# RMS normalization on one core: squares four rows at a time, half of the rows scaled on ScalarE and multiplied on GpSimd, and the code of two engines placed at slot 60

## Chip, cores and metric

One core of a Trainium2 chip; the program is started on that core alone. The metric is device microseconds of one execution. Kernels that are compared ran on the same chip in alternating rounds.

## The reference

```python
batch, seq, dim = 16, 1024, 512            # x: float32; gamma: ones(512)
rms = np.sqrt(np.mean(x ** 2, axis=-1, keepdims=True) + 1e-5)
return (x / rms * gamma).astype(np.float32)
```

That is 16384 rows of 512 numbers: 33.55 MB to read and 33.55 MB to write. Every row is touched once, and the arithmetic is small.

## The kernel before

The rows are cut into 4 tiles of 128 partitions x 32 rows (8.39 MB each), which live in three buffers ("slots" in the kernel's names, not to be confused with the code slots of the change). Eight rows (a group) are worked on at a time. All loads and stores of x are issued from SyncE, in this order; each covers all 128 partitions:

```python
    load(0, 0, 0, 8); load(0, 0, 8, 16); load(0, 0, 16, 32); load(1, 1, 0, 32)
    ...
    def transfers(t, g):                    # called after a group is done
        if (t, g) == (0, 0):
            store(0, 0, 0, 1)               # one-row stores between the loads of tile 2
            load(2, 2, 0, 16)
            store(0, 0, 1, 2)
            load(2, 2, 16, 24)
            store(0, 0, 2, 3)
            load(2, 2, 24, 32)
        elif (t, g) == (0, 24):  store(0, 0, 3, 32)
        elif (t, g) == (1, 8):   store(1, 1, 0, 16); load(3, 0, 0, 16); load(3, 0, 16, 32)
        elif (t, g) == (1, 24):  store(1, 1, 16, 32)
        elif (t, g) == (2, 24):  store(2, 2, 0, 32)
        elif (t, g) == (3, 8):   store(3, 0, 0, 16)
        elif (t, g) == (3, 24):  store(3, 0, 16, 32)
```

So there are 18 transfers of x. The arithmetic of a group:

```python
    # row_stats: sums of squares; two kinds of group alternate
    #   odd groups:  ScalarE squares 4 rows into PSUM, VectorE reduces them    (x2)
    #   even groups: ScalarE squares one row and accumulates its sum           (x8)
    nc.scalar.activation(out=rms, in_=ss, func=AF.Sqrt, bias=eps_t, scale=1.0 / D)
    nc.vector.reciprocal(out=rstd, in_=rms)
    # apply: for each of the 8 rows, on VectorE: row = row * rstd * gamma
    nc.vector.scalar_tensor_tensor(out=..., in0=..., scalar=rstd[:, r : r + 1],
                                   in1=gamma_b, op0=OP.mult, op1=OP.mult)
```

Of the kernel before, what the change touches and what calls it, by code (L numbers as in the profile page):

```python
# [1 line left out]

# [4 lines left out]


@with_exitstack
def kernel(  # L10
    ctx: ExitStack,
    tc: tile.TileContext,
    x: bass.AP,
    gamma: bass.AP,
    out: bass.AP,
):
    nc = tc.nc
    P = nc.NUM_PARTITIONS
    eps = 1e-5
    fp32 = mybir.dt.float32  # L20
    AF = mybir.ActivationFunctionType
    OP = mybir.AluOpType

    xf = x.flatten_outer_dims()
    of = out.flatten_outer_dims()
    N, D = xf.shape
    R = 32
    G = 8
    H = 4
    assert N == 4 * P * R  # L30

    xv = xf.rearrange("(t p r) d -> t p r d", p=P, r=R)
    ov = of.rearrange("(t p r) d -> t p r d", p=P, r=R)

    const = ctx.enter_context(tc.tile_pool(name="const", bufs=1))
    stats = ctx.enter_context(tc.tile_pool(name="stats", bufs=4))
    psum = ctx.enter_context(tc.tile_pool(name="psum", bufs=2, space=bass.MemoryType.PSUM))

    slots = [const.tile([P, R, D], fp32, name=f"slot{i}") for i in range(3)]

    def load(t, slot, r0, r1):
        nc.sync.dma_start(out=slots[slot][:, r0:r1], in_=xv[t][:, r0:r1])

    def store(t, slot, r0, r1):
        nc.sync.dma_start(out=ov[t][:, r0:r1], in_=slots[slot][:, r0:r1])

    load(0, 0, 0, 8)
    load(0, 0, 8, 16)
    load(0, 0, 16, 32)
    load(1, 1, 0, 32)  # L50

    gamma_row = const.tile([1, D], fp32)
    nc.scalar.dma_start(out=gamma_row, in_=gamma.unsqueeze(0))
    ones_col = const.tile([1, P], fp32)
    nc.vector.memset(ones_col, 1.0)  # L55
    gamma_psum = psum.tile([P, H, D], fp32, name="sq")
    nc.tensor.matmul(gamma_psum[:, 0], ones_col, gamma_row, start=True, stop=True)  # L57
    gamma_b = const.tile([P, D], fp32)
    nc.vector.tensor_copy(out=gamma_b, in_=gamma_psum[:, 0])  # L59

    eps_t = const.tile([P, 1], fp32)
    nc.vector.memset(eps_t, eps)  # L62
    sq_scratch = const.tile([P, D], fp32)

    def row_stats(slot, g):
        ss = stats.tile([P, G], fp32, name="ss")
        rms = stats.tile([P, G], fp32, name="rms")
        rstd = stats.tile([P, G], fp32, name="rstd")
        if (g // G) % 2:
            for h in range(0, G, H):  # L70
                sq = psum.tile([P, H, D], fp32, name="sq")
                nc.scalar.activation(out=sq, in_=slots[slot][:, g + h : g + h + H, :], func=AF.Square)  # L72
                nc.vector.tensor_reduce(  # L73
                    out=ss[:, h : h + H], in_=sq, axis=mybir.AxisListType.X, op=OP.add
                )
        else:
            for r in range(G):
                nc.scalar.activation(  # L78
                    out=sq_scratch,
                    in_=slots[slot][:, g + r, :],  # L80
                    func=AF.Square,
                    accum_out=ss[:, r : r + 1],
                )
        nc.scalar.activation(out=rms, in_=ss, func=AF.Sqrt, bias=eps_t, scale=1.0 / D)  # L84
        nc.vector.reciprocal(out=rstd, in_=rms)  # L85
        return rstd

    def apply(slot, g, rstd):
        for r in range(G):
            nc.vector.scalar_tensor_tensor(  # L90
                out=slots[slot][:, g + r, :],
                in0=slots[slot][:, g + r, :],
                scalar=rstd[:, r : r + 1],
                in1=gamma_b,
                op0=OP.mult,
                op1=OP.mult,
            )

    groups = [(t, g) for t in range(4) for g in range(0, R, G)]
    slot_of = [0, 1, 2, 0]  # L100

    def transfers(t, g):
        if (t, g) == (0, 0):
            store(0, 0, 0, 1)
# [5 lines that stand above are left out]
        elif (t, g) == (0, 24):  # L110
            store(0, 0, 3, 32)
        elif (t, g) == (1, 8):
            store(1, 1, 0, 16)
            load(3, 0, 0, 16)
            load(3, 0, 16, 32)
        elif (t, g) == (1, 24):
            store(1, 1, 16, 32)
        elif (t, g) == (2, 24):
            store(2, 2, 0, 32)
        elif (t, g) == (3, 8):  # L120
            store(3, 0, 0, 16)
        elif (t, g) == (3, 24):
            store(3, 0, 16, 32)

    ahead = row_stats(0, 0)
    for k, (t, g) in enumerate(groups):
        rstd = ahead
        if k + 1 < len(groups):
            tn, gn = groups[k + 1]
            ahead = row_stats(slot_of[tn], gn)  # L130
        apply(slot_of[t], g, rstd)
        transfers(t, g)


# [1 line left out]
_INS = ['x', 'gamma']  # L136
_OUTS = [((16, 1024, 512), 'float32')]


# [23 lines left out]
```

## Time and profile before

| | before |
|---|---|
| time, median of 3 runs | 162.62 us (162.05 to 162.84) |
| span of the profiled run | 160.3 us |
| VectorE / ScalarE busy | 122.6 us (76%) / 80.1 us (50%) |
| data moved | 67.11 MB, 97.8% of the 16 DMA engines' time |

97.8% of 160.3 us is 156.8 us for each DMA engine on average. The kernel moves data nearly all the time, and no arithmetic can help unless a transfer waits for it.

The costliest groups of instructions (line, engine, operation, shapes, count; then busy us and mean ns of one; then idle time just before):

```profile
L90 DVE SCALAR_TENSOR_TENSOR slot<-slot,rstd,gamma_b 128x512 f32<-128x512 f32 x128 | 85.7, 738 | 0.1
L78 ACT ACTIVATE sq_scratch<-slot 128x512 f32<-128x512 f32 x64 | 40.0, 625 | 16.0 <-DMA slot<-in_x_dram 14.7
L73 DVE TENSOR_REDUCE ss<-sq 128x4 f32<-128x2048 f32 x16 | 36.0, 2274 | 10.1 <-ACT sq L72 10.0
L72 ACT ACTIVATE sq<-slot 128x2048 f32<-128x2048 f32 x16 | 29.8, 1862 | 8.1 <-DVE ss L73 8.1
```

What SyncE waited for when it issued transfers (total us, times, longest):

```profile
SPq L45 <- DVE slot L90: 102.3, 5, 27.5
SPq L158 <- DMA out_dram<-slot: 16.4, 1, 16.4
...
```

The second of these lines is the wait from the last store's issue to its landing. It is much longer than the store itself needs (4.19 MB are 9.8 us at 428 GB/s, which is 67.11 MB in the 156.8 us), so an earlier store was still under way: the arithmetic is several us ahead of the DMA even at the end.

The last stretches of the span, with the busy time of each engine (all zero by then), and in the last two columns the DMA share and GB/s. A packet is counted here in the stretch in which it starts.

```profile
core 0: us, PE busy (x) PEld busy (x) DVE busy (x) ACT busy (x) POOL busy (x), PEclk, DMA share, GB/s
157.50:158.00 0.50, 0.00 (x0) 0.00 (x0) 0.00 (x0) 0.00 (x0) 0.00 (x0) 1.00 0.16 66
158.00:158.50 0.50, 0.00 (x0) 0.00 (x0) 0.00 (x0) 0.00 (x0) 0.00 (x0) 1.00 0.01 0
158.50:159.00 0.50, 0.00 (x0) 0.00 (x0) 0.00 (x0) 0.00 (x0) 0.00 (x0) 1.00 0.00 0
159.00:160.00 1.00, 0.00 (x0) 0.00 (x0) 0.00 (x0) 0.00 (x0) 0.00 (x0) 1.00 0.00 0
```

After 158.0 us no data packet starts any more.

### The profile page before, as it was taken

How to read it: one execution, taken by the hardware profiler on the slowest of the kernel's cores; microseconds unless marked ns; L12 is line 12 of the kernel's file. 1: busy time of each engine (PE TensorE's matmuls, PEld its weight loads, DVE VectorE, ACT ScalarE, POOL GpSimd, SP SyncE). 2: the span in 40 equal slices, each digit the busy share in tenths (PEclk: the TensorE clock that was granted, in tenths of full speed). 3: DMA queues.
4: the chain of work that ended last, by engine and by line, in shares of the span. 5: the costliest groups of instructions: out<-in, count | busy, mean ns of one | idle time of the engine just before them, and what ended most of it. 6: DMA issues, size and time to landing. Idle time of an engine off the chain costs nothing.

```text
span 160.3 us, 415 instructions
## 1 busy us (share of the span) xinstructions
PE 2.0 (1%) x2; PEld 0.5 (0%) x2; DVE 122.6 (76%) x163; ACT 80.1 (50%) x162; POOL 0.2 (0%) x4
## 2 busy tenths in 40 slices
PE   4000000000000000000000000000000000000000
PEld 1000000000000000000000000000000000000000
DVE  0102999999995199999999999999999999950000
ACT  3099739900499999969009600796099400000000
POOL 0000000000000000000000000000000000000000
DMA  6999999969799999998899999999999799799993
GB/s 197 437 413 523 392 392 523 523 262 523 327 403 407 456 435 503 474 444 356 385 441 466 401 409 490 401 401 499 409 515 474 327 507 458 335 392 450 458 401 139
DMA packets 2597, 67.13 MB, mean 419 GB/s; under 512 B 290, under 2 KB 290, under 8 KB 675
## 3 DMA queue, kind: packets, MB, share of 16 engines
q1 hardware_dynamic: 2592, 67.11, 97.8%
q14 instruction: 3, 0.02, 0.0%
q10 hardware_dynamic: 2, 0.00, 0.0%
HBM read 33.56 MB, written 33.55 MB: 419 GB/s over the span
## 4 chain that ended last, share of the span: by engine, by line
DVE 69%; ACT 12%; DMA 4%; issue 2%; DVEq 0%
DVE slot L90 51%; DVE ss L73 17%; ACT sq_scratch L78 7%; ACT sq L72 4%; DMA slot<-in_x_dram 4%; DVE rstd L85 1%; ACT rms L84 1%; DVEq L158 0%
## 5 line engine op out<-in xcount | busy, mean ns | idle before, releaser
L90 DVE SCALAR_TENSOR_TENSOR slot<-slot,rstd,gamma_b 128x512 f32<-128x512 f32 x128 | 85.7, 738 | 0.1
L78 ACT ACTIVATE sq_scratch<-slot 128x512 f32<-128x512 f32 x64 | 40.0, 625 | 16.0 <-DMA slot<-in_x_dram 14.7
L73 DVE TENSOR_REDUCE ss<-sq 128x4 f32<-128x2048 f32 x16 | 36.0, 2274 | 10.1 <-ACT sq L72 10.0
L72 ACT ACTIVATE sq<-slot 128x2048 f32<-128x2048 f32 x16 | 29.8, 1862 | 8.1 <-DVE ss L73 8.1
L84 ACT ACTIVATE rms<-ss,eps_t 128x8 f32<-128x8 f32 x16 | 4.6, 298 | 26.6 <-DVE ss L73 26.4
L78 ACT ACTIVATION_READ_ACCUMULATOR sq_scratch<-slot 128x1 f32 x64 | 11.9, 187 | 0.0
L85 DVE RECIPROCAL rstd<-rms 128x8 f32<-128x8 f32 x16 | 3.1, 192 | 5.7 <-ACT rms L84 5.7
L59 DVE COPY gamma_b<-sq 128x512 f32<-128x512 f32 x1 | 0.7, 692 | 3.2 <-PE sq L57 3.2
L57 PE MATMUL sq<-gamma_row,ones_col 1*128 1x512 f32 x2 | 2.0, 1122 | 2.1 <-DMA gamma_row<-in_gamma_dram 2.1
L78 ACT ACT_TABLE_LOAD x1 | 1.3, 1283 | 1.3 <-PEq L147 1.3
L84 ACT ACT_TABLE_LOAD x1 | 1.3, 1283 | 0.0
L55 DVE MEMSET ones_col<- 1x128 f32 x1 | 0.2, 165 | 0.8 <-PEq L147 0.8
L57 PEld LDWEIGHTS sq<-gamma_row,ones_col 1*128 1x128 f32 x2 | 0.5, 306 | 2.1 <-issue 2.1
L147 POOL MEMSET const-bfloat16-1.0<- 128x1 bf16 x1 | 0.1, 101 | 0.0
L147 POOL MEMSET const-uint8-127<- 128x1 uint8 x1 | 0.1, 101 | 0.0
L147 POOL MEMSET const-float32-0.0<- 128x1 f32 x1 | 0.1, 98 | 0.2 <-issue 0.2
L147 POOL MEMSET const-float32-1.0<- 128x1 f32 x1 | 0.1, 98 | 0.0
L62 DVE MEMSET eps_t<- 128x1 f32 x1 | 0.1, 59 | 0.0
## 6 DMA issues: line engine op xcount, KB each, us to landing
slot<-in_x_dram SPq DMA_DIRECT2D x4, 4096.0 KB, 24.7
out_dram<-slot SPq DMA_DIRECT2D x4, 4096.0 KB, 22.5
slot<-in_x_dram SPq DMA_DIRECT2D x4, 2048.0 KB, 11.5
out_dram<-slot SPq DMA_DIRECT2D x1, 7424.0 KB, 35.8
out_dram<-slot SPq DMA_DIRECT2D x3, 256.0 KB, 32.1
gamma_row<-in_gamma_dram ACTq DMA_DIRECT2D x1, 2.0 KB
slot<-in_x_dram SPq DMA_DIRECT2D x1, 40.0
out_dram<-slot SPq DMA_DIRECT2D x1
```

Of the source, the lines that this page charges most:

```text
L55: nc.vector.memset(ones_col, 1.0)
L57: nc.tensor.matmul(gamma_psum[:, 0], ones_col, gamma_row, start=True, stop=True)
L59: nc.vector.tensor_copy(out=gamma_b, in_=gamma_psum[:, 0])
L62: nc.vector.memset(eps_t, eps)
L72: nc.scalar.activation(out=sq, in_=slots[slot][:, g + h : g + h + H, :], func=AF.Square)
L73: nc.vector.tensor_reduce(out=ss[:, h : h + H], in_=sq, axis=mybir.AxisListType.X, op=OP.add)
L78: nc.scalar.activation(out=sq_scratch, in_=slots[slot][:, g + r, :], func=AF.Square, accum_out=ss[:, r : r + 1],)
L84: nc.scalar.activation(out=rms, in_=ss, func=AF.Sqrt, bias=eps_t, scale=1.0 / D)
L85: nc.vector.reciprocal(out=rstd, in_=rms)
L90: nc.vector.scalar_tensor_tensor(out=slots[slot][:, g + r, :], in0=slots[slot][:, g + r, :], scalar=rstd[:, r : r + 1], in1=gamma_b, op0=O ...
L147: nc = _bacc.Bacc("TRN2", target_bir_lowering=False, num_devices=1)
```

## The change

Its intent was to relieve VectorE, the busiest compute engine: ScalarE scales half of the rows and GpSimd multiplies those by gamma; in exchange all sums of squares come from four-row squares on ScalarE and reductions on VectorE. VectorE reads gamma from PSUM, so that it has one SBUF input only. Two lines also ask for a place for the code of ScalarE and VectorE; "slot 60" below is only a name for their argument `offset=60`, and so for other numbers.

```diff
+    nc.scalar.addr_align(128, offset=60, max_nops=0)
+    nc.vector.addr_align(128, offset=60, max_nops=0)
 ... (PSUM buffers, gamma kept in PSUM and in SBUF)
-        if (g // G) % 2: ... else: ...          # two kinds of group
+        for h, home in ((0, psum), (H, const)):
+            sq = home.tile([P, H, D], fp32, name=f"sq{h}")
+            nc.scalar.activation(out=sq, in_=slots[slot][:, g + h : g + h + H, :], func=AF.Square)
+            nc.vector.tensor_reduce(out=ss[:, h : h + H], in_=sq, axis=mybir.AxisListType.X, op=OP.add)
 ...
-        for r in range(G):
+        for r in range(H):
+            nc.scalar.activation(
+                out=x[:, g + r, :], in_=x[:, g + r, :], func=AF.Copy, scale=rstd[:, r : r + 1]
+            )
+        nc.gpsimd.tensor_tensor(
+            out=x[:, g : g + H, :], in0=x[:, g : g + H, :],
+            in1=gamma_b.to_broadcast([P, H, D]), op=OP.mult,
+        )
+        for r in range(H, G):
             nc.vector.scalar_tensor_tensor(
 ...
-                in1=gamma_b,
+                in1=gamma_psum,
```

The 18 transfers of x stay as they were, in the same order.

## The prediction

> **What bounds the kernel now.** The DMA engines. The page's DMA queue part gives queue 1 67.11 MB and 97.8% of 16 engines' span: 0.978 x 160.3 = 156.8 us. The packets in the trace run from about 2.5 us after the span's start to its end, so inside that stretch under 1 us is empty. 67.11 MB in 156.8 us is 428 GB/s[...]. VectorE is 122.6 us busy (76%) and ScalarE 80.1 (50%). The chain of waits is 69% VectorE, but it ends at the last store's issue: in the timeline VectorE ends at 142.5 us, and the waits of the DMA queue show 16.4 us from there to landing. The last store, 4.19 MB, needs only 9.8 us at 428 GB/s, so its data began to move near 150: about 7 us of slack, even at the end.

> **What the change does, costed from the trace.**
> - All squares become 128x2048: 32 x 1.86 us, minus about 0.06 overlap, = 58 us. The 64 ACTIVATEs with accumulator read (64 x 0.75 pitch = 48 us) go. Added: 64 scaled copies of 128x512, estimated 0.65 us each = 41 us. ScalarE: 80 -> about 103 us.
> - VectorE: 16 more reduces of 2.24 us (+36), 64 fewer scalar_tensor_tensor of 0.66 us pitch (-43). 122.6 -> about 116 us. Hardly relieved.
> - GpSimd: 16 multiplies of 128x2048. No duration in the trace; [...]
> - Code placement: off the limit, worth about nothing.
> - DMA: the same 18 transfers in the same order, same sizes.

> **On the critical path: nearly nothing.** Per group (4.19 MB in and out, 9.8 us of DMA) VectorE needs 2 x 2.24 + 0.19 + 4 x 0.66 = 7.3 us, ScalarE about 6.5[...]; all below 9.8. [...] My hand schedule: first rows stored at about 25 us (20.5 before; the loads alone keep the queue full to about 40), tile 0's rest at 47 (45.8), first half of tile 1 at 65 (69), last store issued at about 140 (136 to 146), before the queue empties near 150. So the end does not move.

> **Prediction: 162.4 us, range 161.8 to 163.0.** Faster by over 2%: 0.01. Within 2%: 0.95. Slower by over 2%: 0.04.

> **What would show each step.** Queue 1 again near 156.8 us (97 to 98%) and no empty slice in the DMA row; span 160 to 160.7; VectorE busy 113 to 119, ScalarE 98 to 108[...] us; scalar_tensor_tensor and reduce means unchanged within 5% [...]; the last store issued before 149 us, with the wait from it to landing longer than 9.8 us.

> **What would make it wrong.** GpSimd at 9 us or more per multiply, or GpSimd and VectorE blocking each other so that a group takes over about 8.2 us: then stores come late, the queue runs dry and time grows by several us. In-order waits on ScalarE (scaled copies standing ahead of the next squares) could do the same. [...]

The sum came to nothing added: the terms for a group, 7.3 us for VectorE and about 6.5 us for ScalarE, were all put below the 9.8 us of DMA, so the prediction is the time of before, 162.4 us against 162.62. The 0.65 us of a scaled copy is the author's estimate; the trace of before has 625 ns for an ACTIVATE of the same 128x512 shape. The waits on ScalarE that it feared were small in after: its scaled copies waited 12.2 us in all for rstd, 2.4 us at most.

## More of the kernel before

All runs told of here are at a granted clock of 1.00.

From the page of the profile. The first line is the span. The row DMA has one digit for each fortieth of the span: the mean busy share of the 16 DMA engines in tenths. The queue lines give packets, MB, and the time of the packets as a share of 16 engines' span; queue 1 carries x, and queue 14 is of the kind that the page calls "instruction": its packets are taken here for fetches of the engines' own code.

```profile
span 160.3 us, 415 instructions
...
DMA  6999999969799999998899999999999799799993
...
q1 hardware_dynamic: 2592, 67.11, 97.8%
q14 instruction: 3, 0.02, 0.0%
...
```

At the start, from the timeline (start us, duration us): ScalarE issues the small load of gamma and loads its function table.

```profile
0.72 0.51 ACTq L53 DMA_DIRECT2D gamma_row<-in_gamma_dram  x1
...
1.27 1.28 ACT L78 ACT_TABLE_LOAD   x1 [1.27 <-PEq L147]
...
```

## The result

| | before | after |
|---|---|---|
| time, median of 4 runs | 162.34 us (161.92 to 162.84) | 164.29 us (163.91 to 164.58) |
| span of the profiled run | 160.3 us | 162.5 us |
| VectorE busy | 122.6 us | 115.5 us |
| ScalarE busy | 80.1 us | 105.2 us |
| GpSimd busy | 0.2 us | 72.5 us |

The ratio of after to before is 1.0118, with a 95% interval of 1.0078 to 1.0157: slower by about 1.2%, clear of noise, and outside the range of the prediction. A ratio is always the mean time of one kernel's fast runs over that of the other's of the same rounds, so it is not quite the ratio of the medians quoted beside it.

The page of after:

```profile
span 162.5 us, 360 instructions
...
DMA  6999999999798999999899999999999998899980
...
q1 hardware_dynamic: 2592, 67.11, 96.7%
q14 instruction: 4, 0.03, 0.1%
...
```

Queue 1 moved the same bytes in the same number of packets. Its share of the span fell from 97.8% to 96.7%, because the span grew: 96.7% of 162.5 us is 157.1 us, against 156.8. The DMA row ends in a 0 where it ended in a 3: the last fortieth of the span is nearly empty. Queue 14 has 4 packets where it had 3; one of the 3 is a packet of 32 bytes at the very start, so the 8192-byte packets, of which more below, went from 2 to 4.

The groups of after:

```profile
L88 POOL TENSOR_TENSOR slot<-slot,gamma_b 128x2048 f32<-128x2048 f32 x16 | 72.3, 4525 | 65.9 <-ACT slot L85 64.2
L72 DVE TENSOR_REDUCE ss<-sq 128x4 f32<-128x2048 f32 x32 | 71.3, 2266 | 8.6 <-ACT sq L71 8.6
L71 ACT ACTIVATE sq<-slot 128x2048 f32<-128x2048 f32 x32 | 59.9, 1883 | 8.5 <-DMA slot<-in_x_dram 6.7
L85 ACT ACTIVATE slot<-slot,rstd 128x512 f32<-128x512 f32 x64 | 40.8, 709 | 12.2 <-DVE rstd L79 12.2
L95 DVE SCALAR_TENSOR_TENSOR slot<-slot,rstd,gamma_psum 128x512 f32<-128x512 f32 x64 | 43.5, 740 | 0.2
```

VectorE's arithmetic went as costed: the reduce takes 2266 ns (2274 before) and the scalar_tensor_tensor 740 ns (738 before). GpSimd's multiply takes 4525 ns, and ScalarE's scaled copies took more than costed, 709 ns against an estimate of 650. GpSimd did not slow VectorE's scalar_tensor_tensor: 57 of the 64 instructions of after ran beside a GpSimd multiply and took 740 ns, as did the other 7. Whether gamma's place in PSUM has a part in that was not shown: no run has it elsewhere beside GpSimd's work.

SyncE's waits of after:

```profile
SPq L48 <- DVE slot L95: 72.3, 5, 16.8
SPq L48 <- POOL slot L88: 34.1, 7, 17.3
SPq L165 <- DMA out_dram<-slot: 22.4, 1, 22.4
...
```

The wait from the last store's issue to its landing is now 22.4 us (16.4 before): the arithmetic finished even further ahead of the DMA, and the kernel still ended later. So the last store did not come late. The end of the DMA work is what changed. The last stretches of after, same columns:

```profile
157.50:158.00 0.50, 0.00 (x0) 0.00 (x0) 0.00 (x0) 0.00 (x0) 0.00 (x0) 1.00 0.30 131
158.00:158.50 0.50, 0.00 (x0) 0.00 (x0) 0.00 (x0) 0.00 (x0) 0.00 (x0) 1.00 0.01 0
158.50:159.00 0.50, 0.00 (x0) 0.00 (x0) 0.00 (x0) 0.00 (x0) 0.00 (x0) 1.00 0.15 66
159.00:160.00 1.00, 0.00 (x0) 0.00 (x0) 0.00 (x0) 0.00 (x0) 0.00 (x0) 1.00 0.08 33
```

Here is the loss. After 158.0 us nearly everything is over, as before, but two more packets start. Such a packet is 32768 bytes and takes 1.21 us; one packet in a stretch of 1 us makes 1.21 / 16 = 0.08 of 16 engines, as the last line shows. So one DMA engine of the 16 still starts packets when the other fifteen have none left to start.

The packets in the trace say it exactly. Each transfer ends with a 4-byte packet on each of the 16 engines, and the last 16 of these are the moments at which the 16 engines finished (us, from the first instruction):

```
          first   median   third-last   second-last   last     last - median
before   157.82   158.05      158.34        158.43   158.96       0.92
after    158.06   158.23      158.79        159.18   161.06       2.83
```

The median engine moved by 0.18 us, the last one by 2.10 us. The spans of these two runs differ by 2.15 us.

Packets do not carry the number of their engine, but the recorded start of most packets lies 3 to 4 ns before the recorded end of another. I read the two as neighbours on one engine, and so most of them can be strung together: 2592 / 16 = 162 packets of x for each engine. The string that ends last in after, compared with the median engine after the same transfer:

```
us       what happens on this engine                                behind the median by
 3.82    8192-byte packet of queue 14, 0.31 us;
         the data packet after it takes 0.53 us longer                 0.91 us
39.9     64 KB packet at the turn from loads to stores takes
         1.20 us longer (0.31 to 0.66 on the other engines)            1.69 us
51.4     32 KB packet takes 0.59 us longer                             2.18 us
67.64    8192-byte packet of queue 14, 0.31 us;
         the data packet after it takes 0.37 us longer                 2.85 us
end                                                                   2.83 us
```

Two fetches of instructions fell on one DMA engine. In before there are also two such packets, at 45.8 and 59.8 us, but on two different engines. In after there are four: 1.8, 3.8, 67.6 and 70.3 us. The other two, at 1.8 and 70.3 us, also fell on one engine, and it ended only 0.94 us behind: it was 0.34 us behind after the first load, where the engine above was 0.91.

At the start of after, the timeline shows that ScalarE takes 2.83 us to issue the gamma load and gets to its function table at 4.02 us instead of 1.27:

```profile
1.17 2.83 ACTq L56 DMA_DIRECT2D gamma_row<-in_gamma_dram  x1
...
4.02 1.28 ACT L71 ACT_TABLE_LOAD   x1 [4.02 <-issue]
...
```

### The profile page after: what moved, and what is told of

Its sections match the earlier page's. It is cut to its first block, busy times and chain, and to the rows that moved or that the text cites. A ratio compares the mean times of both kernels' runs of the same rounds, so it can differ in the third digit from the quotient of the medians.

```text
span 162.5 us, 360 instructions
## 1 busy us (share of the span) xinstructions
PE 2.0 (1%) x2; PEld 0.5 (0%) x2; DVE 115.5 (71%) x115; ACT 105.2 (65%) x114; POOL 72.5 (45%) x20
## 3 DMA queue, kind: packets, MB, share of 16 engines
q1 hardware_dynamic: 2592, 67.11, 96.7%
## 4 chain that ended last, share of the span: by engine, by line
DMA 42%; DVE 24%; ACT 10%; issue 3%; POOLq 3%; POOL 3%; ACTq 0%; SPq 0%
DMA out_dram<-slot 23%; DMA slot<-in_x_dram 20%; DVE ss L72 15%; DVE slot L95 8%; ACT sq L71 5%; ACT slot L85 4%; POOLq L165 3%; POOL slot L88 3%; ACT L78 1%; DVE rstd L79 0%; ACTq L165 0%; SPq L45 0%; ACT rms L78 0%; ACTq L71 0%; POOLq L88 0%
## 5 line engine op out<-in xcount | busy, mean ns | idle before, releaser
L88 POOL TENSOR_TENSOR slot<-slot,gamma_b 128x2048 f32<-128x2048 f32 x16 | 72.3, 4525 | 65.9 <-ACT slot L85 64.2
L72 DVE TENSOR_REDUCE ss<-sq 128x4 f32<-128x2048 f32 x32 | 71.3, 2266 | 8.6 <-ACT sq L71 8.6
L71 ACT ACTIVATE sq<-slot 128x2048 f32<-128x2048 f32 x32 | 59.9, 1883 | 8.5 <-DMA slot<-in_x_dram 6.7
L85 ACT ACTIVATE slot<-slot,rstd 128x512 f32<-128x512 f32 x64 | 40.8, 709 | 12.2 <-DVE rstd L79 12.2
L95 DVE SCALAR_TENSOR_TENSOR slot<-slot,rstd,gamma_psum 128x512 f32<-128x512 f32 x64 | 43.5, 740 | 0.2
L62 DVE COPY gamma_b<-gamma_psum 128x512 f32<-128x512 f32 x1 | 0.7, 692 | 8.6 <-PE gamma_psum L60 8.6
L60 PE MATMUL gamma_psum<-gamma_row,ones_col 1*128 1x512 f32 x2 | 2.0, 1122 | 8.1 <-DMA gamma_row<-in_gamma_dram 8.1
L60 PEld LDWEIGHTS gamma_psum<-gamma_row,ones_col 1*128 1x128 f32 x2 | 0.5, 305 | 8.1 <-issue 8.1
```

What stands on the lines that cost most here:

```text
L60: nc.tensor.matmul(gamma_psum, ones_col, gamma_row, start=True, stop=True)
L62: nc.vector.tensor_copy(out=gamma_b[:, 0], in_=gamma_psum)
L71: nc.scalar.activation(out=sq, in_=slots[slot][:, g + h : g + h + H, :], func=AF.Square)
L72: nc.vector.tensor_reduce(out=ss[:, h : h + H], in_=sq, axis=mybir.AxisListType.X, op=OP.add)
L85: nc.scalar.activation(out=x[:, g + r, :], in_=x[:, g + r, :], func=AF.Copy, scale=rstd[:, r : r + 1])
L88: nc.gpsimd.tensor_tensor(out=x[:, g : g + H, :], in0=x[:, g : g + H, :], in1=gamma_b.to_broadcast([P, H, D]), op=OP.mult,)
```

## The theories

**Theory C (compute).** The new arithmetic (GpSimd's and ScalarE's traffic in SBUF, or the longer chain, or ScalarE's late start) slows one DMA engine at the turns between loads and stores.

## The experiments

Twelve kernels, all correct, three calls on three chips; each is compared with the runs of before of its own call (median 162.60, 162.49 and 162.58 us). "Fetches" are the 8192-byte packets of queue 14 that start after the first instruction. In all of these runs the median DMA engine ended between 158.05 and 158.44 us.

| kernel | fetches at, us | last engine behind the median, us | time, median us | ratio to before (95%) |
|---|---|---|---|---|
| before | 45.8, 59.8 | 0.92 | 162.34 | |
| after | 1.8, 3.8, 67.6, 70.3 | 2.83 | 164.29 | 1.0118 (1.0078 to 1.0157) |
| after_no_slot | 59.2, 67.3 | 0.74 | 162.39 | 0.9991 (0.9967 to 1.0016) |
| before_slot60 | 1.8, 3.6, 52.5, 60.9 | 2.76 | 164.41 | 1.0115 (1.0088 to 1.0142) |
| after_slot60_act | 1.8, 59.1, 67.8 | 0.75 | 162.32 | 0.9987 (0.9965 to 1.0009) |
| after_slot60_dve | 3.7, 67.9, 69.7 | 3.22 | 164.58 | 1.0124 (1.0102 to 1.0145) |
| before_extra_early | 49.8, 63.7, and a useless load at 7.3 | 3.92 | 165.48 | 1.0184 (1.0160 to 1.0209) |
| before_extra_late | 46.0, 60.0, and a useless load at 119.3 | 2.46 | 163.79 | 1.0078 (1.0058 to 1.0098) |
| before_extra_small | 47.3, 61.8, and a small useless load at 7.3 | 2.56 | 163.86 | 1.0081 (1.0058 to 1.0104) |
| after_slot100_dve | 39.0, 67.4 | 0.42 | 161.86 | 0.9989 (0.9943 to 1.0035) |
| after_nops110 | 18.3, 27.0 | 2.52 | 163.73 | 1.0069 (1.0047 to 1.0091) |
| after_slot100_both | 21.9, 38.7 | 2.53 | 163.75 | 1.0073 (1.0050 to 1.0096) |
| after_slot122_both | 5.7, 18.1 | 2.83 | 164.29 | 1.0105 (1.0085 to 1.0126) |
| after_no_row_stores | 1.8, 3.7, 68.0, 69.6 | 2.18 | 163.83 | 1.0084 (1.0061 to 1.0107) |

### 1. The change without its placement lines

```diff
-    nc.scalar.addr_align(128, offset=60, max_nops=0)
-    nc.vector.addr_align(128, offset=60, max_nops=0)
```

> The changed kernel without the two code-placement lines. Theory P (placement): the two lines make ScalarE and VectorE fetch code while the data moves, 4 fetches instead of 2, two of them on the same DMA engine; that engine ends 2.8 us after the median engine (0.9 before). Then this run has 2 fetches of 8 KB during the data, the last DMA engine ends 0.5 to 1.2 us after the median one, ScalarE loses its 4.0 us start stall, and time is 162.0 to 162.8 us, within 0.3% of before. Theory C (compute): GpSimd and ScalarE traffic, or the longer chain, slow one DMA engine at the turns from loads to stores; then time stays at 163.9 to 164.6 us and the lag stays above 2 us.

Measured: 162.39 us, ratio 0.9991: all of the loss is gone. From its page:

```profile
span 160.2 us, 357 instructions
...
q1 hardware_dynamic: 2592, 67.11, 97.8%
q14 instruction: 2, 0.02, 0.0%
```

The share of queue 1 is back at 97.8%, the span at 160.2 us, and queue 14 has 2 packets. The whole change of the arithmetic, by itself, is worth nothing measurable: VectorE was off the limit. Theory C expected 163.9 us or more and falls.

### 2. The kernel of before with the placement lines alone

```diff
+    nc.scalar.addr_align(128, offset=60, max_nops=0)
+    nc.vector.addr_align(128, offset=60, max_nops=0)
```

> The kernel of before with only the two code-placement lines added. Theory P: 4 or more fetches during the data, a branch at the start of ScalarE and VectorE, one DMA engine 2 to 3 us behind the median at the end, time 163.6 to 164.6 us (0.8 to 1.4% slower than before). Theory C: 162.0 to 162.8 us, no change.

Measured: 164.41 us, ratio 1.0115, the same loss as the full change, with not one arithmetic instruction altered. Its page:

```profile
span 162.4 us, 418 instructions
...
q1 hardware_dynamic: 2592, 67.11, 96.6%
q14 instruction: 4, 0.03, 0.1%
```

### 3. Which engine's code it is

```diff
 after_slot60_act:   keeps nc.scalar.addr_align(...), drops nc.vector.addr_align(...)
 after_slot60_dve:   drops nc.scalar.addr_align(...), keeps nc.vector.addr_align(...)
```

> The changed kernel with only ScalarE's code placed at slot 60. Theory P: 3 fetches during the data; tells which engine's fetches hit the DMA engine that ends last. If ScalarE's do: lag about 2.5 us and 163.6 to 164.4 us; if VectorE's do: lag about 1 us and 162.2 to 163.0 us, without ScalarE's start stall gone. Theory C: 163.9 to 164.6 us.

> The changed kernel with only VectorE's code placed at slot 60. Theory P: the mirror of the ScalarE-only run: one of the two stays near 162.5 us, the other holds most of the 1.9 us. Theory C: 163.9 to 164.6 us in both.

Measured: with ScalarE's line alone 162.32 us, no loss; with VectorE's alone 164.58 us, the whole loss. ScalarE's line still delays ScalarE (its function table comes at 3.58 us) and still adds a fetch, at 1.8 us; but data first moves at 1.74 us, and here the last engine ends only 0.75 us behind. VectorE's line adds a fetch at 3.7 us, amid the first load. So ScalarE's late start, which I had thought of as a cause of its own, costs nothing. The last stretches with ScalarE's line alone:

```profile
158.50:159.00 0.50, 0.00 (x0) 0.00 (x0) 0.00 (x0) 0.00 (x0) 0.00 (x0) 1.00 0.00 0
159.00:160.00 1.00, 0.00 (x0) 0.00 (x0) 0.00 (x0) 0.00 (x0) 0.00 (x0) 1.00 0.00 0
```

And with VectorE's line alone:

```profile
158.00:158.50 0.50, 0.00 (x0) 0.00 (x0) 0.00 (x0) 0.00 (x0) 0.00 (x0) 1.00 0.01 0
158.50:159.00 0.50, 0.00 (x0) 0.00 (x0) 0.00 (x0) 0.00 (x0) 0.00 (x0) 1.00 0.15 66
159.00:160.00 1.00, 0.00 (x0) 0.00 (x0) 0.00 (x0) 0.00 (x0) 0.00 (x0) 1.00 0.00 0
160.00:161.00 1.00, 0.00 (x0) 0.00 (x0) 0.00 (x0) 0.00 (x0) 0.00 (x0) 1.00 0.08 33
```

Again single packets where the other engines are done, one of them started after 160 us.

### 4. A delay of one DMA engine without any code fetch

If the last of 16 engines sets the time, a useless load on one engine must do the same. Here a load of 17 partitions ran on one engine: the traces of these kernels show its 17 packets one after another, and queue 1 counts 2610 packets where it had 2592, so the load has one closing 4-byte packet where each transfer of x has 16. The 27 GB/s of one engine in the expectation below is a packet of x, 32768 bytes in 1.21 us.

```diff
 before_extra_early:
     load(0, 0, 0, 8)
+    nc.sync.dma_start(out=extra, in_=xf[0:34].rearrange("(p r) d -> p (r d)", r=2))   # 17 x 4 KB
 before_extra_late:
             store(1, 1, 16, 32)
+            nc.sync.dma_start(out=extra, in_=...)                                     # the same load
 before_extra_small:
     load(0, 0, 0, 8)
+    nc.sync.dma_start(out=extra, in_=xf[0:17, 0:256])                                 # 17 x 1 KB
```

> The kernel of before plus one useless load of 17 rows of 4 KB (70 KB) straight after the first load; [...] it should run on one DMA engine alone, about 2.6 us at the 27 GB/s that one engine shows. Theory P (the last of the 16 DMA engines sets the time, and an engine that falls behind early falls further behind where loads turn to stores): that engine is 2.6 us behind at once, 3 to 4.5 us at the end, and time is 164.2 to 166 us. Rival A (a delay on one engine is absorbed, only total bytes count): 162.6 to 163 us. Rival B (behind, but it does not grow): 164.2 to 164.7 us, with the lag at the end as at the start.

> The same useless load, but issued behind the last store of tile 1, so it moves near 110 to 120 us, past the turns between loads and stores. Theory P: the engine ends 2.6 us (3.5 if it is the one that fetches code as well) after the median, 0.9 before, so time is 1.6 to 2.7 us longer than before: 164.0 to 165.2 us, and less than with the early load. Rival A: 162.6 to 163 us.

> The kernel of before with a small useless load on one DMA engine, 17 rows of 1 KB, about 0.7 to 0.9 us, at 7.3 us: as much as an early fetch of code costs, with no fetch. If any engine that is 0.7 to 0.9 us behind before the turn from loads to stores falls further behind there: 2 to 3 us behind at the end, 163.5 to 164.8 us. If the growth belongs to the fetches: 0.7 to 1.2 us behind at the end (1.5 if it is also VectorE's fetch engine), 162.2 to 163.1 us.

Measured: the late load took 2.64 us on its engine, and that kernel's last engine ended 2.46 us behind; 163.79 us, a little under the expected range. Its 0.07 MB, spread over 16 engines, would be 0.16 us at 428 GB/s; the delay on one engine cost 1.3 us of time (163.79 against 162.49). The early load took 3.7 us (nine of its packets ran slower than the 159 ns of the others); its engine was 3.7 us behind at 16 us and ended 3.92 us behind, 165.48 us. So this lag was there at once and grew by only 0.25 us; by itself this run does not tell growth from none.

The small early load is the sharpest of the three: it took 0.72 us, moved 17 KB, and its kernel's last engine ended 2.56 us behind, 163.86 us:

```profile
158.50:159.00 0.50, 0.00 (x0) 0.00 (x0) 0.00 (x0) 0.00 (x0) 0.00 (x0) 1.00 0.00 0
159.00:160.00 1.00, 0.00 (x0) 0.00 (x0) 0.00 (x0) 0.00 (x0) 0.00 (x0) 1.00 0.08 33
```

One packet still starts after 159 us, as in after. Strung together as above, the packets show that neither of this kernel's fetches (47.3 and 61.8 us) fell on the engine of the useless load; their engines ended 1.2 and 0.7 us behind. So the growth from under 1 us to over 2 us seen in after does not belong to code fetches. In both kernels an engine that was 0.7 to 0.9 us behind early lost more than another 1 us in the stretch where loads turn to stores (1.3 us between 39 and 55 us in after, by its string of packets; 1.5 us here between 22 and 63 us, and 0.4 us more between 100 and 110 us, where the loads of tile 3 end). The engine that was 3.7 us behind lost less there, and the delay at 119 us, after the last load, did not grow at all.

### 5. Other slots: can the fetches be put where they do no harm?

The expectations below rested on guesses at when a slot asks for its fetch. No run here shows such a rule.

```diff
 after_slot100_dve:   nc.vector.addr_align(128, offset=100, max_nops=0)     # VectorE only
 after_nops110:       both engines: addr_align(128, offset=110, max_nops=128)
 after_slot100_both:  both engines: addr_align(128, offset=100, max_nops=0)
 after_slot122_both:  both engines: addr_align(128, offset=122, max_nops=0)
```

> The changed kernel with only VectorE placed, at slot 100. [...] no fetch near 3.7 us, but the mid-run fetch comes [...] near 10 to 20 us, before the turn from loads to stores, so that engine is 0.7 us behind early and 1.5 to 2.5 at the end: 163.0 to 164.3 us. If any branch costs the fetch: one near 3.7 us too, and 164.3 us or more. If the slot does not matter: 162.4 us.

> The changed kernel with ScalarE's and VectorE's code moved to slot 110 [...]. Theory P: [...] their fetches come before or with the first data (below 3 us) [...]: no fetch between 5 and 125 us, the last DMA engine ends under 0.6 us after the median, and time is 161.4 to 162.2 us, 0.2 to 0.6% faster than before. If the fetches come at 3 to 8 us instead, the lag grows as at slot 60 and time is 163.5 to 164.5 us.

> The changed kernel with ScalarE and VectorE both placed at slot 100. VectorE's fetch came at 38.96 us there and cost its DMA engine nothing; ScalarE's should move from 67.4 to 35 to 42 us as well. If both fall at or after 38.9 us: the last engine ends 0.2 to 0.6 us after the median, 161.6 to 162.2 us, 0.2 to 0.6% faster than before. If ScalarE's falls before the turn at 38.8 us: its engine is 1.5 to 2.5 us behind, 163.0 to 164.3 us.

> The changed kernel with both placed at slot 122[...]. If the fetch [...] goes out with the branch, near 1 to 1.8 us, before data moves: no other fetch before 130 us, last engine under 0.5 us behind, 161.5 to 162.1 us. If it goes out [...] at 4 to 12 us: about 2.5 us behind, 163.5 to 164.6 us.

Measured: my model of when a slot asks for its fetch was poor. Slot 100 for VectorE gave its fetch at 39.0 us (expected 10 to 20), for ScalarE at 21.9 us (expected 35 to 42); the lines with offset 110 and max_nops=128 gave 18.3 and 27.0 us (expected below 3), slot 122 gave 5.7 and 18.1. What held in all of them is what follows from the moment of a fetch. Every kernel with a fetch between 3.6 and 27 us ended with its last engine 2.2 to 3.2 us behind and took 0.7 to 1.2% longer than before. Every kernel without a useless load whose fetches came before 2 us or from 39.0 us on (at or past the turn from loads to stores) stayed within 0.92 us and at the time of before. In after_slot100_both the fetch at 38.7 us did no visible harm beside the one at 21.9.

The strings of packets sharpen this. Two fetches on one engine are not needed: in after_slot122_both the engine that ended 2.83 us behind carried only the fetch at 5.7 us. And it is the lag that counts, not the fetch: in the same kernel the fetch at 18.1 us fell on an engine that was 0.3 us ahead of the median, left it 0.3 us behind, and that engine ended 0.1 us behind.

That VectorE's placement line brings the early fetch whatever its slot is ruled out: after_slot100_dve has the line, with offset=100, and no fetch near 3.7 us (its fetches came at 39.0 and 67.4 us).

after_slot100_dve is the best of all kernels by its median, 161.86 us. Five of its six runs took 161.72 to 162.41 us and one 164.09; with that run in, its ratio of 0.9989 is not shown to be a gain. One reading is that its fetch at 39.0 us sits at the edge of the turn and fell before it in that run; that run has no trace, so this is only argued.

### 6. Without the one-row stores among the loads

```diff
-            store(0, 0, 0, 1)
             load(2, 2, 0, 16)
-            store(0, 0, 1, 2)
             load(2, 2, 16, 24)
-            store(0, 0, 2, 3)
             load(2, 2, 24, 32)
 ...
-            store(0, 0, 3, 32)
+            store(0, 0, 0, 32)
```

> The changed kernel (slot 60) without the three one-row stores that stand between the loads of tile 2; row 0 to 2 go out with the rest of tile 0. The early fetch stays. If the growth at 39 to 60 us comes from the small stores among the loads: the engine stays 0.9 us behind until the fetch near 67.6 us and ends 1.5 to 2.0 us behind, 162.8 to 163.5 us. If it comes from the turn itself (now near 58 us): 2.3 us or more behind, 163.8 to 164.6 us.

Measured: 163.83 us, last engine 2.18 us behind the median: between the two readings. The growth between 39 and 55 us did vanish, but a growth of 0.5 us came at the turn itself, now near 60 us (the fetch at 68.0 us on the same engine added 0.7). So the small stores are part of it and not all of it. Inconclusive on the mechanism.

## Why the prediction was wrong

- "What bounds the kernel now. The DMA engines." Right: the arithmetic of after alone leaves the time at 0.9991.
- VectorE "about 116 us", "Hardly relieved", ScalarE "about 103 us". Right: 115.5 and 105.2 us. GpSimd was busy for 72.5 us, and the VectorE instruction that took 738 ns took 740 beside it.
- First rows stored at about 25 us, tile 0's rest at 47, last store issued at about 140. Right: 26.2, 47.4 and about 139 us.
- "Code placement: off the limit, worth about nothing." This is the step that failed. I looked for its cost on the compute engines, where indeed it costs nothing. It cost 1.9 us on the DMA engines: a fetch of 8 KB at 3.8 us put one of them 0.9 us behind, and that grew to 2.8 us, as broken down below; the placement lines alone, on the kernel of before, took 164.41 us.
- "DMA: the same 18 transfers in the same order, same sizes." True, but not all that the DMA engines carry: the fetches of code at 3.82 and 67.64 us stand in the same string as packets of x.
- "So the end does not move." It rested on 16 engines taken as one. The mean time per engine did stay (156.8 and 157.1 us), and so did the median engine; the end is the last engine's, and that moved by 2.1 us.
- "Queue 1 again near 156.8 us (97 to 98%)": the time held, the share did not (96.7%), and the row of DMA had a nearly empty last slice. These were the signs that the prediction itself had named. (It has the packets run from about 2.5 us to the span's end; they run from 1.74 to 158.96 us. Nothing rests on this.)

How the lag breaks down in after: 0.9 us from the early fetch, 1.3 us from the stretch where loads turn to stores, 0.7 us from the second fetch on the same engine; 2.8 us against the 0.9 us by which the last engine lagged before, which makes the 1.9 us.

What stays open: why an engine that is slightly behind falls further behind at the turn, and how a slot sets the moment of the fetch.

## What to carry to other kernels

In this kernel, with the DMA engines 97.8% full, the time went with the last of the 16: two fetches of 8 KB on one of them, the first at 3.8 us, went with 1.9 us more time, where 7 us of work taken off VectorE brought nothing. Look at when the last DMA packets start, one engine at a time, and not only at the mean share; a share that falls while the bytes stay the same was the sign here. Try code placement alone, apart from the change that it comes with, and check where its instruction fetches land in time.
